# Where three top-k selections stand between one block's norm, its routing and the next stage in a 512-token decoder layer

## Chip, cores and metric

The kernel runs on one core of one Trainium2 chip. The metric is device time in microseconds, the median of several executions. TensorE (PE) multiplies, VectorE (DVE) and ScalarE (ACT) work elementwise, GpSimd (POOL) issues the indirect gathers, SyncE (SP) issues the plain loads.

## What is computed

One decoder layer on 512 tokens of width 1024: a mixing sublayer of sparse attention and a gated recurrence (HGRN2), then a feed-forward sublayer (PEER) in which each token picks 8 x 16 of 16384 single-neuron experts. The reference, cut to what matters here:

```python
# attention: each query keeps the 128 keys with the best indexer score
logits = relu(einsum('bqhd,bsd->bqhs', qi, k_idx))
score  = einsum('bqhs,bqh->bqs', logits, wi)
_, sel = top_k(where(causal, score, -inf), 128)
...
h = _layer_norm(ALPHA * x + concat([att_out, hg_out]) @ w_out, ln1_g, ln1_b)
# PEER
q = h @ w_q ; s = einsum('thpd,hpkd->thpk', q, sub_keys)
s_top, i_top = top_k(s, 16)
best, pos = top_k(pairwise sums of s_top, 16)        # -> experts, gates
hid = gelu(einsum('td,thkd->thk', x, u[experts]))
ffn = einsum('thk,thkd->td', softmax(best) * hid, v[experts])
x = _layer_norm(ALPHA * h + ffn, ln2_g, ln2_b)
```

## The kernel before

Tokens lie in four blocks of 128 (one token a partition). The mixing part runs in two stages, and the PEER part of the blocks is done in two ways.

`stage([0])` computes recurrence and attention of block 0, then index keys and index queries of blocks 1 to 3, `index_scores(1)`, the output projection with the first norm of block 0 (`mix_norm`), then `index_scores(2)` and `choose(1)`, `choose(2)`, then the queries and the top-k lists of block 0's PEER (`queries`, `routing`), which end in lists of indices `idx0_0` and `idx0_1` (line L622). `stage([1, 2, 3])` does the same for the other three blocks together: `index_scores(3)` and `choose(3)`, four recurrence projections (`hf`, `hq`, `hi`, `hg`), the recurrence block by block (`hgrn`), attention block by block, `mix_norm`, `queries`. After it blocks 2 and 3 go through a dense form of PEER that streams all experts, a loop over 128 key rows which TensorE bounds; block 1's experts are gathered beside it.

`index_scores(b)` has eight matmuls, eight copies on ScalarE (tile `rl`) and eight sums on DVE (L411) into the tile `isc`. `choose(b)` has 16 steps on that tile, each a MAX of eight values (L420) and a MATCH_REPLACE that marks them (L421), and a mask at the end; the tile is 256, 384 or 512 columns wide for block 1, 2 or 3. The attention of a block reads the mask with each head's scores (L443, tile `P`).

The PEER of block 0 gathers. A *row* is one expert slot for 128 tokens: POOL issues an indirect DMA of 128 x 1024 floats (L641, 0.524 MB) into one of nine buffers, and DVE takes the dot product with the block's tokens (L665, tile `gu`, 128 u rows) or adds the weighted row (L678, tile `gv`, 76 v rows). These 204 rows are handed out by `pump(n)`: whoever calls it puts the next n rows there in program order. Calls stand in `choose` (1 row at each step), between the loads of each projection (`PUMP` has the number by place), in the recurrence, between the heads of attention (4), in `mix_norm` (2) and in `queries`. While no rows are listed yet (all of stage 0) `pump` does nothing.

Instructions are issued in an order that a scheduler makes from the program and a cost model of its own. `tc.keep_in_program_order(ins)` pins one instruction: it stands behind whatever was written before it on its engine. Rows and many loads are pinned, most else is free, so the scheduler may move a selection step up or down past other work.

The norm (`layer_norm`) has sums, L143 (subtract the mean, times the weight), a root worked out in eleven small steps on 128 x 1 (L115 to L120), and L144 (times the root, plus the bias). Queries and routing of a block read its result, tile `hs`. In the section of rows, L131 is the sum for the norm, L493 the output projection, L525 the queries.

In the changed kernel four lines are added ahead, so L143 and L144 keep their numbers, the score sums are L411, MAX is L422, MATCH_REPLACE L425, attention's scores L447, a u row L669, a v row L682.

Of the kernel before, what the change touches and what calls it, by code (L numbers as in the profile page):

```python
# [15 lines left out]
ALU = mybir.AluOpType  # L16
# [16 lines left out]
STB = 6  # L33
PJ = 16

PUMP = {"cw": 0, "qi": 0, "hf": 4, "hq": 4, "hi": 4, "hg": 3, "qa": 2, "hgrn": 2, "att": 4, "mix": 2, "sel": 1,
        "q0": 7, "q1": 0, "q2": 0, "q3": 0}

PEK1 = 14
# [12 lines left out]
def tile_decoder_layer(ctx, tc, a, out):  # L52
    nc = tc.nc
# [32 lines left out]
    caus = pre.tile([128, 512], F32, name="caus")  # L86
# [184 lines left out]
    def hgrn(b, pr, mixT):  # L271
# [20 lines left out]
        if b:  # L292
            pump(PUMP["hgrn"])
        kt = k2(f"kt{b}")
# [104 lines left out]
        for i, b in enumerate(blocks):  # L399
            pr[b][key] = [t[:, i * 128:(i + 1) * 128] for t in ts_]  # L400

    def index_scores(b, pr):
        nk = (b + 1) * 128
        sc = pre.tile([128, 512], F32, name=f"isc{b}", tag="isc", bufs=3)[:, :nk]
        for h in range(8):
            ip = bank(f"ip{b}_{h}")
            lo = (h % 2) * 64
            nc.tensor.matmul(ip[:, :nk], pr["qi"][h // 2][lo:lo + 64, :], kiT[lo:lo + 64, :nk], start=True, stop=True)
            rl = k2(f"rl{b}_{h}")
            nc.scalar.activation(rl[:, :nk], ip[:, :nk], AF.Relu)  # L410
            nc.vector.scalar_tensor_tensor(sc, rl[:, :nk], pr["widx"][:, h:h + 1],  # L411
                                           caus[:, 512 - nk:] if h == 0 else sc, op0=ALU.mult, op1=ALU.add)
        return sc

    def choose(b, sc):

        m8 = pre.tile([128, 8], F32, name=f"m8_{b}", tag="m8", bufs=2)
        for i in range(16):
            pump(PUMP["sel"])
            nc.vector.max(m8, sc)  # L420
            nc.vector.match_replace(sc, m8, sc, GONE)  # L421
        nc.vector.tensor_scalar(sc, sc, -2e38, BIG, op0=ALU.is_gt, op1=ALU.mult)  # L422
        return sc
# [422 lines left out]
    def stage(blocks, xT):  # L846
        mixT = pre.tile([128, 8, 128 * len(blocks)], F32, name=f"mixT{blocks[0]}", tag="mixT",
                        padded_shape=[128, 8, 384])
        if blocks == [0]:
            pr = {}  # L850
# [8 lines left out]
            pens = {0: pen0}  # L859
        else:  # L860
            pr = index["pr"]
            pens = dict(index["sc"])
            pens[3] = choose(3, index_scores(3, pr[3]))
            kv_norm(blocks, pr)
            hp = hgrn_proj(blocks, xT)
        for i, b in enumerate(blocks):
# [10 lines left out]
            index["sc"] = {1: index_scores(1, index["pr"][1])}  # L877
        mix_norm(blocks, mixT)
        if blocks == [0]:
            index["sc"][2] = index_scores(2, index["pr"][2])  # L880
            for b in (1, 2):
                index["sc"][b] = choose(b, index["sc"][b])
        hT = pre.tile([128, 8, 128 * len(blocks)], F32, name=f"hT{blocks[0]}", tag="mixT",
                      padded_shape=[128, 8, 384])
        queries(blocks, hT)
# [13 lines left out]
    index = {}  # L899
# [55 lines left out]
```

## Time and profile before

| | before |
|---|---|
| time, median of 3 executions | 1598.87 us (1594.95 to 1606.39) |
| time of the profiled execution | 1608.33 us |
| its span | 1606.6 us |
| PE busy | 1450.4 us (90%) |
| DVE busy | 1385.0 us (86%) |
| ACT busy | 708.2 us (44%) |
| POOL busy | 672.9 us (42%) |
| DMA | 467.89 MB, mean 291 GB/s |

The page cuts the span into 40 slices of about 40 us and gives the busy share of an engine in each in tenths. Other views give the busy time of each engine in a stretch, groups of instructions of a line, the waits of an engine by what ended them, and a timeline. The places on the timeline that matter: block 0's norm at 122 to 136 us, its first gather at 197, attention of block 1 from 385 on, the output projection of blocks 1 to 3 from 491 to 521, their norms to 543.5, the dense loop from about 840 to the end.

### The profile page before, as it was taken

The page shows a single profiled execution, that of the slowest core. Times are in us where ns is not written, and L with a number is a line of the kernel's source. Part 1 is how long each engine was busy: PE and PEld are TensorE (multiplying, and loading weights), DVE is VectorE, ACT ScalarE, POOL GpSimd, SP SyncE. Part 2 cuts the span into 40 slices and gives each one's busy share as a digit, 9 for nine tenths or more (in the row PEclk, how much of TensorE's full clock was granted, in tenths as well). Part 3 has the DMA queues.
Part 4 walks back from the last instruction along what each step waited for, and adds up shares of the span by engine and source line. Part 5 has one row for each costly group of instructions (what it writes and reads, how often), then busy time and mean ns, then how long its engine had stood idle before and what let it go on. Part 6 is the DMA issues. An engine that isn't in the chain of part 4 may idle for free. (4 is left out here: it accounts for less than half of the span.)

```text
span 1606.6 us, 24502 instructions
## 1 busy us (share of the span) xinstructions
PE 1450.4 (90%) x7858; PEld 1088.9 (68%) x7858; DVE 1385.0 (86%) x3263; ACT 708.2 (44%) x1502; POOL 672.9 (42%) x531
## 2 busy tenths in 40 slices
PE   8997999757888599679989999999999999999996
PEld 4756544444443366246668888888888889988895
DVE  4219999789898989988887899998998899999998
ACT  3312321223430113169994555555555555555553
POOL 0000057858875610255433444444443344544440
PEclk9998999755799799899999999999999999999998
DMA  8445499889899860467778999999999999999995
GB/s 291 172 154 178 134 388 341 324 296 342 309 336 372 305 244 21 146 201 225 227 238 308 342 347 339 350 355 341 350 354 340 326 348 359 364 334 341 352 365 190
DMA packets 166161, 467.89 MB, mean 291 GB/s; under 512 B 18576, under 2 KB 18704, under 8 KB 165904
## 3 DMA queue, kind: packets, MB, share of 16 engines
q0 software_dynamic: 73728, 268.47, 48.0%
q1 hardware_dynamic: 92304, 197.86, 34.1%
q8 instruction: 62, 1.02, 0.2%
q14 instruction: 67, 0.55, 0.1%
HBM read 464.16 MB, written 2.10 MB: 290 GB/s over the span
## 5 line engine op out<-in xcount | busy, mean ns | idle before, releaser
L641 POOL DMA_INDIRECT gu<-in_u_dram,idx x256 | 328.5, 1283 | 423.4 <-DVE gu L665 212.5
L641 POOL DMA_INDIRECT gv<-in_v_dram,idx x256 | 333.8, 1304 | 401.4 <-DVE hs L678 226.8
L665 DVE SCALAR_TENSOR_TENSOR gu<-gu,hs 128x1024 f32<-128x1024 f32 x256 | 310.7, 1236 | 33.6 <-DMA gu<-in_u_dram,idx 32.6
L678 DVE SCALAR_TENSOR_TENSOR hs<-gv,gate,hs 128x1024 f32<-128x1024 f32 x204 | 261.5, 1282 | 13.5 <-DMA gv<-in_v_dram,idx 11.8
L774 ACT CAST v_0h<-v 128x512 fp32r<-128x512 f32 x128 | 79.7, 623 | 97.4 <-PE acc L805 58.5
L774 ACT CAST v_1h<-v 128x512 fp32r<-128x512 f32 x128 | 79.5, 621 | 93.1 <-DMA v<-in_v_dram 54.3
L525 PE MATMUL pq<-hT,wpq 128*128 128x128 f32 (+1 forms) x512 | 118.5, 389 | 0.0
L776 DVE TENSOR_TENSOR u_0l<-u,u_0h 128x512 fp32r<-128x512 f32 x128 | 88.5, 691 | 26.5 <-ACT u_0h L774 23.8
L774 ACT CAST u_0h<-u 128x512 fp32r<-128x512 f32 x128 | 79.3, 619 | 65.0 <-PE hp L785 34.0
L805 PE MATMUL acc<-v_0h,wl 128*128 128x512 f32 x256 | 102.0, 398 | 3.4 <-DVE wl L795 3.2
L776 DVE TENSOR_TENSOR v_1l<-v,v_1h 128x512 fp32r<-128x512 f32 x128 | 87.9, 687 | 18.6 <-ACT v_1h L774 18.0
L805 PE MATMUL acc<-v_0h,wh 128*128 128x512 f32 x256 | 101.0, 394 | 0.0
L525 PEld LDWEIGHTS pq<-hT,wpq 128*128 128x128 f32 x512 | 79.3, 196 | 31.9 <-issue 1.8
L774 ACT CAST u_1h<-u 128x512 fp32r<-128x512 f32 x128 | 79.4, 621 | 47.4 <-PE acc L805 41.0
L805 PE MATMUL acc<-v_1h,wl 128*128 128x512 f32 x256 | 99.9, 390 | 0.1
L805 PE MATMUL acc<-v_1h,wh 128*128 128x512 f32 x256 | 99.7, 389 | 0.0
L805 PE MATMUL acc<-v_0l,wh 128*128 128x512 f32 x256 | 99.5, 390 | 0.0
L776 DVE TENSOR_TENSOR u_1l<-u,u_1h 128x512 fp32r<-128x512 f32 x128 | 87.7, 685 | 5.0 <-ACT wh L793 3.0
L776 DVE TENSOR_TENSOR v_0l<-v,v_0h 128x512 fp32r<-128x512 f32 x128 | 88.2, 689 | 3.7 <-ACT v_0h L774 2.8
L785 PE MATMUL hp<-hTl,u_0h 128*128 128x256 f32 x512 | 83.8, 286 | 6.6 <-ACT u_0h L774 6.6
L785 PEld LDWEIGHTS hp<-hTl,u_0h 128*128 128x128 f32 x512 | 76.4, 189 | 19.3 <-ACT u_0h L774 10.9
L785 PE MATMUL hp<-hTh,u_1l 128*128 128x256 f32 x512 | 84.6, 287 | 5.1 <-DVE u_1l L776 4.9
(275 smaller groups left out, 3154.6 us busy)
## 6 DMA issues: line engine op xcount, KB each, us to landing
v<-in_v_dram SPq DMA_DIRECT2D x256, 256.0 KB, 5.9
u<-in_ut_dram SPq DMA_DIRECT2D x256, 256.0 KB, 6.0
wpq<-in_w_pq_dram SPq DMA_DIRECT2D x32, 512.0 KB, 4.9
wo<-in_w_o_dram SPq DMA_DIRECT2D x16, 512.0 KB, 5.3
hfw<-in_w_hf_dram SPq DMA_DIRECT2D x8, 512.0 KB, 4.9
hqw<-in_w_hq_dram SPq DMA_DIRECT2D x8, 512.0 KB, 5.4
hiw<-in_w_hi_dram SPq DMA_DIRECT2D x8, 512.0 KB, 6.3
qaw<-in_w_qa_dram SPq DMA_DIRECT2D x8, 512.0 KB, 5.8
```

The costliest lines, as they stand in the source:

```text
L525: nc.tensor.matmul(qp[:, :nt], w[:, k, :], hT[:, k, :nt], start=(k == 0), stop=(k == 7))
L641: nc.gpsimd.indirect_dma_start(out=t, out_offset=None, in_=table, in_offset=bass.IndirectOffsetOnAxis(ap=idx[b][k // 64][:, k % 64:k % 64 ...
L665: nc.vector.scalar_tensor_tensor(g, g, 1.0, hs[b], op0=ALU.mult, op1=ALU.mult, accum_out=hd[:, k:k + 1]))
L678: nc.vector.scalar_tensor_tensor(hs[b], g, gate[:, b, k:k + 1], hs[b], op0=ALU.mult, op1=ALU.add))
L774: nc.scalar.copy(h, x)
L776: nc.vector.tensor_tensor(l, x, h.bitcast(F32), op=ALU.subtract)
L785: nc.tensor.matmul(hp, ut[:, k * 128:(k + 1) * 128], ht[n][:, k, :], start=(n + q + k == 0), stop=(n == 1 and q == 2 and k == 3))
L805: nc.tensor.matmul(acc[i][n], wt[:, sl], vt, start=(j == 0 and q == 0), stop=(j == 127 and q == 2))
```

## The change

```diff
--- before.py
+++ after.py
@@ -33,7 +33,7 @@
 STB = 6
 PJ = 16
 
-PUMP = {"cw": 0, "qi": 0, "hf": 4, "hq": 4, "hi": 4, "hg": 3, "qa": 2, "hgrn": 2, "att": 4, "mix": 2, "sel": 1,
+PUMP = {"cw": 0, "qi": 0, "hf": 3, "hq": 3, "hi": 3, "hg": 3, "qa": 2, "hgrn": 2, "att": 4, "mix": 2, "sel": 1,
         "q0": 7, "q1": 0, "q2": 0, "q3": 0}
 
 PEK1 = 14
@@ -399,7 +399,7 @@
         for i, b in enumerate(blocks):
             pr[b][key] = [t[:, i * 128:(i + 1) * 128] for t in ts_]
 
-    def index_scores(b, pr):
+    def index_scores(b, pr, behind=False):
         nk = (b + 1) * 128
         sc = pre.tile([128, 512], F32, name=f"isc{b}", tag="isc", bufs=3)[:, :nk]
         for h in range(8):
@@ -408,16 +408,20 @@
             nc.tensor.matmul(ip[:, :nk], pr["qi"][h // 2][lo:lo + 64, :], kiT[lo:lo + 64, :nk], start=True, stop=True)
             rl = k2(f"rl{b}_{h}")
             nc.scalar.activation(rl[:, :nk], ip[:, :nk], AF.Relu)
-            nc.vector.scalar_tensor_tensor(sc, rl[:, :nk], pr["widx"][:, h:h + 1],
-                                           caus[:, 512 - nk:] if h == 0 else sc, op0=ALU.mult, op1=ALU.add)
+            ins = nc.vector.scalar_tensor_tensor(sc, rl[:, :nk], pr["widx"][:, h:h + 1],
+                                                 caus[:, 512 - nk:] if h == 0 else sc, op0=ALU.mult, op1=ALU.add)
+            if behind and h == 0:
+                tc.keep_in_program_order(ins)
         return sc
 
-    def choose(b, sc):
+    def choose(b, sc, behind=False):
 
         m8 = pre.tile([128, 8], F32, name=f"m8_{b}", tag="m8", bufs=2)
         for i in range(16):
             pump(PUMP["sel"])
-            nc.vector.max(m8, sc)
+            ins = nc.vector.max(m8, sc)
+            if behind and i == 0:
+                tc.keep_in_program_order(ins)
             nc.vector.match_replace(sc, m8, sc, GONE)
         nc.vector.tensor_scalar(sc, sc, -2e38, BIG, op0=ALU.is_gt, op1=ALU.mult)
         return sc
@@ -860,7 +864,8 @@
         else:
             pr = index["pr"]
             pens = dict(index["sc"])
-            pens[3] = choose(3, index_scores(3, pr[3]))
+            pens[2] = choose(2, pens[2], behind=True)
+            pens[3] = choose(3, index_scores(3, pr[3]), behind=True)
             kv_norm(blocks, pr)
             hp = hgrn_proj(blocks, xT)
         for i, b in enumerate(blocks):
@@ -877,9 +882,9 @@
             index["sc"] = {1: index_scores(1, index["pr"][1])}
         mix_norm(blocks, mixT)
         if blocks == [0]:
-            index["sc"][2] = index_scores(2, index["pr"][2])
-            for b in (1, 2):
-                index["sc"][b] = choose(b, index["sc"][b])
+
+            index["sc"][2] = index_scores(2, index["pr"][2], behind=True)
+            index["sc"][1] = choose(1, index["sc"][1], behind=True)
         hT = pre.tile([128, 8, 128 * len(blocks)], F32, name=f"hT{blocks[0]}", tag="mixT",
                       padded_shape=[128, 8, 384])
         queries(blocks, hT)
```

In words: (1) the first score sum of block 2 and the first selection step of block 1 are pinned, so that none of them is issued before block 0's norm is through. (2) The selection of block 2 moves from there to the start of the next stage, behind block 0's routing, and is pinned; since rows are listed by then, each of its 16 steps now calls for a row. The selection of block 3 is pinned behind it. (3) The three projections `hf`, `hq` and `hi` call for three rows a place in place of four: `hf` to `hi` give up twelve rows.

What this does to the issue order is seen at three places on DVE. The first is block 0's norm; `hs_104` is the block's tokens, `isc_695` and `isc_799` are the score tiles of blocks 1 and 2, `rs_tl`, `rs_yl` and `vel` belong to the root. Before:

```order
L143 SCALAR_TENSOR_TENSOR hs_104<-hs_104,mvl_0_777,ln_0_0_763 128x1024
L411 SCALAR_TENSOR_TENSOR isc_799<-rl_0_802,cw_619,caus 128x384
L420 MAX m_1_840<-isc_695 128x8
L115 TENSOR_SCALAR rs_tl_0_785<-vel_0_782 128x1
L411 SCALAR_TENSOR_TENSOR isc_799<-rl_1_807,cw_619,isc_799 128x384
L421 MATCH_REPLACE isc_695<-m_1_840,isc_695 128x256
L116 TENSOR_SCALAR rs_yl_0_784<-rs_tl_0_785 128x1
```

and after:

```order
L118 TENSOR_TENSOR rs_tl_0_785<-vel_0_782,rs_yl_0_784 128x1
L119 SCALAR_TENSOR_TENSOR rs_tl_0_785<-rs_tl_0_785,rs_yl_0_784 128x1
L120 SCALAR_TENSOR_TENSOR rs_yl_0_784<-rs_tl_0_785,rs_yl_0_784 128x1
L144 SCALAR_TENSOR_TENSOR hs_104<-hs_104,rs_yl_0_784,ln_0_1_765 128x1024
L411 SCALAR_TENSOR_TENSOR isc_799<-rl_0_802,cw_619,caus 128x384
L411 SCALAR_TENSOR_TENSOR isc_799<-rl_1_807,cw_619,isc_799 128x384
```

The score sums of block 2 and the selection of block 1 stood between the steps of the root; now the root's steps follow each other and L144 comes before the first score sum.

The second place is where attention of block 1 begins (tile `P`, its first head); `gu` are u rows of block 0 with their number behind the name, L327 and L328 are the recurrence. Before:

```order
L665 SCALAR_TENSOR_TENSOR gu_94_2144,hd_1466<-gu_94_2144,hs_104 128x1024
L328 TENSOR_TENSOR S_3_2557<-S_3_2557,ds_3_2548 128x256
L665 SCALAR_TENSOR_TENSOR gu_95_2147,hd_1466<-gu_95_2147,hs_104 128x1024
L351 TENSOR_TENSOR o_2566<-o_0_2569,gs_1929 128x4x64
L443 ISA P_0_2748,nmx_2743<-sp_0_2746,isc_695 128x256
```

and after:

```order
L328 TENSOR_TENSOR S_3_2569<-S_3_2569,ds_3_2560 128x256
L669 SCALAR_TENSOR_TENSOR gu_116_2391,hd_1391<-gu_116_2391,hs_104 128x1024
L669 SCALAR_TENSOR_TENSOR gu_117_2394,hd_1391<-gu_117_2394,hs_104 128x1024
L351 TENSOR_TENSOR o_2578<-o_0_2581,gs_1941 128x4x64
L447 ISA P_0_2760,nmx_2755<-sp_0_2758,isc_695 128x256
```

Rows are counted from 0: 96 stood ahead of the first score, now 118.

The third place is the norm of block 1 in the second stage (`hs_3192` before, `hs_3204` after; `mix` is the output projection, L496 or L500 adds it). Before, v rows of block 0 (`gv`) stand between the norms' steps, about every third instruction:

```order
L134 TENSOR_SCALAR vel_2_3343<-mvl_2_3338 128x1
L118 TENSOR_TENSOR rs_tl_1_3314<-vel_1_3311,rs_yl_1_3313 128x1
L143 SCALAR_TENSOR_TENSOR hs_3194<-hs_3194,mvl_2_3338,ln_1_0_3292 128x1024
L678 SCALAR_TENSOR_TENSOR hs_104<-gv_48_3262,gate,hs_104 128x1024
L115 TENSOR_SCALAR rs_tl_2_3346<-vel_2_3343 128x1
L119 SCALAR_TENSOR_TENSOR rs_tl_1_3314<-rs_tl_1_3314,rs_yl_1_3313 128x1
L496 SCALAR_TENSOR_TENSOR hs_3196<-hs_3196,mix_1_3360 128x512
L678 SCALAR_TENSOR_TENSOR hs_104<-gv_49_3265,gate,hs_104 128x1024
```

After:

```order
L500 SCALAR_TENSOR_TENSOR hs_3206<-hs_3206,mix_1_3340 128x512
L132 BN_AGGR mvl_1_3318<-stl_1_0_3319 128x2
L682 SCALAR_TENSOR_TENSOR hs_104<-gv_59_3301,gate,hs_104 128x1024
L131 BN_STATS stl_2_0_3351<-hs_3206 128x6
L134 TENSOR_SCALAR vel_1_3323<-mvl_1_3318 128x1
L143 SCALAR_TENSOR_TENSOR hs_3204<-hs_3204,mvl_1_3318,ln_1_0_3304 128x1024
L131 BN_STATS stl_3_0_3383<-hs_3208 128x6
L132 BN_AGGR mvl_2_3350<-stl_2_0_3351 128x2
```

The 60th v row (`gv_59`) is the last until the three norms are through. From the 60th v row to the end of the program DVE's order is otherwise that of before.

## Rows read from the trace of the kernel before

**Rows 1.** The page's part 2: TensorE's busy tenths in 40 slices of the span.
```profile
PE   8997999757888599679989999999999999999996
```
**Rows 2.** Stretches: length; PE, PEld, DVE, ACT, POOL busy (count); clock; DMA share; GB/s.
```profile
123.40:197.00 73.60, 59.43 (x354) 45.34 (x353) 73.60 (x368) 17.13 (x42) 0.00 (x0) 0.88 0.45 151
197.00:276.30 79.30, 78.47 (x255) 37.16 (x253) 73.21 (x159) 19.82 (x29) 49.11 (x43) 1.00 0.98 362
276.30:384.80 108.50, 71.96 (x529) 49.06 (x530) 94.65 (x190) 24.67 (x71) 78.46 (x64) 0.64 0.88 312
384.80:490.90 106.10, 86.70 (x288) 43.33 (x288) 96.70 (x168) 40.76 (x96) 83.52 (x70) 0.80 0.92 330
490.90:521.00 30.10, 29.36 (x64) 12.68 (x64) 23.70 (x29) 0.00 (x0) 13.56 (x12) 0.94 1.00 385
521.00:543.50 22.50, 4.01 (x17) 3.14 (x16) 22.22 (x54) 2.35 (x4) 14.02 (x10) 0.61 0.88 303
543.50:578.40 34.90, 34.71 (x119) 21.98 (x120) 28.06 (x25) 5.93 (x12) 20.62 (x18) 0.91 0.95 357
```
**Rows 3.** Timeline of DVE at block 0's norm: start, duration (us), instruction.
```profile
122.18 1.27 DVE L143 SCALAR_TENSOR_TENSOR hs<-hs,mvl,ln 128x1024 f32<-128x1024 f32 x1
134.65 1.27 DVE L144 SCALAR_TENSOR_TENSOR hs<-hs,rs_yl,ln 128x1024 f32<-128x1024 f32 x1
137.55 0.87 DVE L420 MAX8 m<-isc 128x8 f32<-128x384 f32 x2
139.26 0.87 DVE L420 MAX8 m<-isc 128x8 f32<-128x384 f32 x2
```
**Rows 4.** DVE's groups by shape, 123.4 to 197 us: count | busy us, mean ns.
```profile
L420 DVE MAX8 m<-isc 128x8 f32<-128x384 f32 x16 | 8.7, 546 | 0.0
L420 DVE MAX8 m<-isc 128x8 f32<-128x256 f32 x16 | 6.5, 407 | 0.0
```
**Rows 5.** Timeline of ACT and POOL: first query scores copied, first gather issued.
```profile
149.72 0.59 ACT L534 COPY pss<-psc 128x512 f32<-128x512 f32 x1 [2.64 <-PE psc L529]
197.38 1.15 POOL L641 DMA_INDIRECT gu<-in_u_dram,idx  x1 [120.12 <-DVE idx L622]
```
**Rows 6.** DVE's waits, 197 to 545 us: total us, times, longest.
```profile
DVE gu L665 <- DMA gu<-in_u_dram,idx: 13.0, 11, 2.9
DVE P L443 <- PE sp L441: 7.9, 8, 2.9
```
**Rows 7.** Rows and gathers by line: duration ns min/median/max, first and last start.
```profile
L665 DVE SCALAR_TENSOR_TENSOR gu<-gu,hs x59: 1209/1219/2974, 275.1 to 383.3; 128x1024 f32<-128x1024 f32 x59
L641 POOL DMA_INDIRECT gu<-in_u_dram,idx x112: 937/989/1988, 200.1 to 399.8; - x112
```
**Rows 8.** Timeline of DVE: first score, last rows, mixing output, rows between norms.
```profile
384.77 0.41 DVE L443 CUSTOM_DVE_ANT_0 P<-sp,isc 128x256 f32<-128x256 f32 x1
...
478.91 12.08 DVE L678 SCALAR_TENSOR_TENSOR hs<-gv,gate,hs 128x1024 f32<-128x1024 f32 x9
490.90 0.68 DVE L472 TENSOR_TENSOR mixT<-oT,rT 128x512 f32<-128x512 f32 x1
...
520.77 1.27 DVE L678 SCALAR_TENSOR_TENSOR hs<-gv,gate,hs 128x1024 f32<-128x1024 f32 x1
...
538.25 1.28 DVE L678 SCALAR_TENSOR_TENSOR hs<-gv,gate,hs 128x1024 f32<-128x1024 f32 x1
...
540.90 0.16 DVE L120 SCALAR_TENSOR_TENSOR rs_yl<-rs_tl,rs_yl 128x1 f32<-128x1 f32 x1
541.09 0.16 DVE L118 TENSOR_TENSOR rs_tl<-vel,rs_yl 128x1 f32<-128x1 f32 x1
...
542.26 1.28 DVE L144 SCALAR_TENSOR_TENSOR hs<-hs,rs_yl,ln 128x1024 f32<-128x1024 f32 x1
```
**Rows 9.** Timeline of PE: first transpose of the normed tokens, with its wait.
```profile
536.93 1.97 PE L213 MATMUL hT_ps<-ident,hs 128*128 128x128 f32 x8 [15.86 <-DVE rs_tl L115]
```

## The prediction

> **What bounds the kernel now.** I read the busy tenths of the page first, then the table of stretches, then the order of DVE, and last the timeline at the places where the order changes. TensorE is full from about the twentieth slice to the end [rows 1], and the 34.9 us in which the queries of blocks 1 to 3 start on TensorE hold 34.71 us of its work [rows 2]. From there on nothing in the change is left except four rows of block 0 that move ahead of that point, so a microsecond gained or lost before it is gained or lost at the end. I call that point N: the last normalized block of stage [1,2,3], 542.26 + 1.28 = 543.5 us [rows 8].
>
> Between block 0's norm and N the engine to watch is DVE. It is busy for 73.60 of 73.60 us up to the first gather, then 73.21 of 79.30, 94.65 of 108.50, 96.70 of 106.10, 23.70 of 30.10 and 22.22 of 22.50 [rows 2]. So 384.1 us of its work stand in 420.1 us, 36 us are idle, and the question of the whole change is whether N moves by more or less than the work and the idle time on this one engine. The idle time was ended mostly by gather DMAs (13.0 us for u rows) and by score matmuls (7.9 us) [rows 6]. Where TensorE waits, DVE is the releaser: before N it waits 15.86 us for the norms [rows 9].
>
> **Part 1: the norm of block 0 is freed.** Before, L143 stands at 122.18 and L144, which ends the norm, at 134.65 [rows 3], because the small steps of the inverse root are dealt out among block 2's score sums and the first selection steps. After, these stand alone. There are eleven, and where they run alone they follow each other at 541.09 − 540.90 = 0.19 us [rows 8], so L144 comes at about 123.45 + 11 × 0.195 + 0.2 = 125.8 instead of 134.65, some 9 us earlier, and TensorE's queries with it.
>
> Block 1's and block 2's selections alternate before: one pair of steps takes 139.26 − 137.55 = 1.71 us [rows 3]. Split by the durations of their MAX, 546 against 407 ns [rows 4], a step of block 2 is 0.98 us, and its sixteen steps 15.7 us. They leave the stretch up to the first gather, and about one step of block 3's selection (1.3 us) goes with them. Three things come back: 1.4 us of waiting inside the inverse root, about 3 us because the score sums and block 1's steps now depend on each other back to back, and a wait for the first query scores. ScalarE copies these until 149.72 + 0.59 = 150.3 [rows 5]; 9 us earlier is 141.3, and DVE is ready for them at about 139.5, so 2 us. The first list of indices, and the first gather, come 15.7 + 1.3 − 6.4 = 10.6 us earlier: about 186.8 instead of 197.38 [rows 5].
>
> **Part 2: the selection of block 2 goes in front of stage [1,2,3].** From the first gather to the start of block 1's attention DVE now has everything it had, plus that selection (15.7 us, and 0.7 for its start and its mask). The place of 276.3 is where attention's inputs are built; up to it two rows fewer are pumped, 38 to 36 (−2.3), and 2 us of block 3's selection fall on the far side. Work 73.2 + 15.7 + 0.7 + 1.3 − 2.3 − 2 + 1.6 for dependent steps = 88.2, idle 2 to 3 us (before 6.1: the selection steps fill part of what waited for gathers): 91. 186.8 + 91 = 277.8 against 276.3. The 10.6 us of part 1 are already spent: **+1.5**.
>
> **Part 3: more rows stand ahead of block 1's attention.** This carries the sum. The sixteen rows that the moved selection pumps exceed the twelve that the three projections give up, and the scheduler packs them early: ahead of the first score of block 1, at 384.77 [rows 8], stood 96 rows, now 118. In 276.3 to 384.8 that is 59 rows before and 83 after, 24 more, at 1.219 us, the median of a u row [rows 7]: 29.3 us. With 2.7 us of block 3's selection behind 276.3, DVE's work is 94.65 + 32 = 126.6 us. The idle time of this stretch was 13.9 us, and rows now fill most of it; I keep 2.4 (bounds 0 and 13.9). So 129 instead of 108.5, **+20.5**; block 1's attention starts at 407 instead of 385.
>
> Can the gathers keep up? A row is 0.524 MB; 83 rows and about 3.5 MB of weights are 47 MB. The best rate that a stretch shows is 385 GB/s [rows 2], which gives 122 us, just under the 126.6 of DVE. In the Trainium skill, "DMA: Bandwidth & Descriptors", section "Where 436 GB/s comes from", the ceiling of the fabric is 435 GB/s; by that the same bytes would take an estimated 108 us and the sum stays as it is. No stretch here comes above 385.
>
> **Part 4: what is given back.** From block 1's first score to the last block's attention output (490.90 [rows 8]) 54 rows stand instead of 66. Almost all that go are in block 3's attention. But there the last nine rows (478.91, 12.08 us [rows 8]) run beside a chain over TensorE and ScalarE which ends only 0.9 us before the output does, so dropping them gains that 0.9 and perhaps 3 us of single rows that stand between two scores: **−4** (bounds −8 and +2). The output projection then is TensorE's, 29.36 of 30.10 [rows 2]; it has about four more rows beside it with the DMA share already 1.00, 4 × 0.524 MB / 385 GB/s = 5.4 us at worst, nothing at best: **+2**. Last, ten rows between 520.77 and 538.25 [rows 8] stand among the three norms behind the projection; after, all rows of this place are ahead of the last sum, and the norms run alone: ten rows less, 12 us: **−12**. Behind N there are 16 rows instead of 20 beside TensorE's queries, which are not waiting for them: 0 (to −2).
>
> Sum: 1.5 + 20.5 − 4 + 2 − 12 = **+8 us** at N, and at the end. A second way: DVE has 384.1 us before and four more rows (4.7 us) plus 5 us of dependent steps after, with an idle time of 36 before and 34 after: +8 as well, and with idle of 27 to 45, −1 to +19. The profiled execution took 1608.3 us by its own time, 0.6% above the median of 1598.9; 8 us on the median are 1607.
>
> Two ACT table loads fall away and the input loads of the three blocks go some places earlier on SP's queue. ScalarE is busy 24.67 of 108.50 us where it matters [rows 2], so this costs nothing; if attention waited for ScalarE, the loads would be worth 2 to 3 us together.
>
> **Rivals.**
> - *Faster.* The 22 extra rows ahead of block 1's attention cost only what was idle there: if DVE's idle 13.9 us take twelve of them and the TensorE work of that stretch (71.96 us at a clock of 0.64 [rows 2]) sets the pace, part 3 is +5 to 10 in place of 20.5, and N comes 3 to 8 us early; with block 3's attention closing up fully (−8) and no loss in the projection, 10 to 16 early. It decides once the stretch takes under 118 us. Against it: the 32 us are counted from the order, and the idle time was made by score and gather waits which don't vanish. Time 1583 to 1596.
> - *Slower.* The gathers starve. A gather issue takes 937 ns at best, 989 in the median and 1988 at worst, and a u row up to 2974 ns where it waits behind something [rows 7]. With the selection steps now between the rows, issues may come at 1.4 us a row and more, and the 83 rows of part 3 then take 83 × 1.4 = 116 us where 83 × 1.219 = 101 are counted: +15 on top. It decides when the rows' mean spacing exceeds 1.3 us. POOL has 78.46 busy of 108.50 [rows 2], which leaves room, so it is less likely. The Trainium skill, "SBUF — State Buffer", section "SBUF: two separate sides", says that DVE in a two-port mode or with two SBUF inputs shuts GpSimd out of the shared pair for a whole instruction, which delays descriptors; by that rule a denser DVE makes issues slower. The longest issue above fits it, but the median says that it is rare. Time 1615 to 1630.
> - *The change doesn't do what it says.* TensorE's queries are not ready when DVE is, the first gather stays near 192 to 197, and part 2 is +7 to +12 rather than +1.5. Against it: the queries' weights are loaded by then, and the scores were waiting for the norm. Time 1612 to 1618.
>
> **How the numbers follow.** The forecast (N later by 2 to 14 us) has 0.50; N within −6 and +2, since attention closes up more, 0.17; the faster rival 0.10; starved gathers 0.15; late queries 0.08. The time is that of the forecast, 1607 (its own range 1601 to 1613). The range of 1591 to 1624 leaves 0.08 below and 0.08 above. A measurement here can tell about 1% from no change, 16 us, so faster has 0.07 (below 1583: most of the faster rival's lower half), slower 0.22 (above 1615: starved gathers, and the upper edge of forecast and late queries), the same 0.71.
>
> **What would show it.** Part 1: L144 of block 0 near 126 and the first gather near 187. Part 2: the place of 276.3 at 277 to 279. Part 3: the first score of block 1 near 407, with DVE over 95% busy in the 110 us before. Part 4: the time from the last projection matmul to N at 10 to 11 us instead of 22. If the first score of block 1 comes before 397, part 3 was too dear and the faster rival is at work; if gather waits ahead of it exceed 15 us, the slower one. N compared with the end tells whether what lies behind N really only shifts.

## The result, and the profile of the changed kernel

The changed kernel takes 1621.7 us (median of 4 executions, 1616.35 to 1629.42) beside 1596.91 us (4 executions, 1594.08 to 1606.39) for the kernel before: a ratio of 1.0142, 95% interval 1.0106 to 1.0178, so 17 to 28 us slower. The forecast was 1607 and slower, the range reached to 1624. The sign and the range held; the size did not: 24.8 us were lost where 8 were forecast, and "slower", by more than 1%, had a chance of only 0.22.

The profiled executions are 1606.6 and 1620.5 us long, 13.9 us apart. The table of stretches of the changed kernel, with cuts at the same events as [rows 2] (the columns are those of [rows 2]; the fifth stretch is the fifth and sixth there, and the sixth runs from the last norm to the last list of indices, 157.70 us before):

```profile
123.40:185.70 62.30, 58.46 (x357) 44.52 (x356) 59.55 (x315) 17.09 (x42) 0.00 (x0) 0.97 0.53 179
185.70:276.20 90.50, 87.60 (x284) 42.62 (x282) 87.61 (x198) 18.95 (x28) 49.58 (x47) 1.00 0.90 328
276.20:410.40 134.20, 65.27 (x508) 46.09 (x508) 121.81 (x246) 25.60 (x73) 100.14 (x79) 0.55 0.90 321
410.40:517.40 107.00, 82.84 (x282) 42.73 (x278) 85.70 (x137) 38.71 (x92) 71.15 (x60) 0.83 0.87 305
517.40:559.40 42.00, 31.41 (x80) 15.35 (x80) 36.67 (x71) 2.36 (x5) 19.62 (x16) 0.89 0.83 313
559.40:714.90 155.50, 137.80 (x444) 76.41 (x445) 140.99 (x816) 37.17 (x71) 39.57 (x32) 0.96 0.45 148
```

The first three stretches are those of block 0's norm and queries, of the rows up to attention's inputs, and of the rows up to block 1's first score. The first is 11.3 us shorter than before, the second 11.2 longer, the third 25.7 longer; DVE is still 91% busy in it. Attention (the fourth) takes 107.0 us beside 106.1, though DVE has 11 us less to do in it, so its idle time there grew from 9.4 to 21.3 us. Projection and norms are 10.6 us shorter. The last normalized block of stage [1,2,3] ends at 559.4 instead of 543.5.

From the timelines of DVE and POOL, the events that the prediction named (start, duration, instruction):

```profile
125.82 1.28 DVE L144 SCALAR_TENSOR_TENSOR hs<-hs,rs_yl,ln 128x1024 f32<-128x1024 f32 x1
185.73 1.26 POOL L645 DMA_INDIRECT gu<-in_u_dram,idx  x1 [108.12 <-DVE pos L576]
410.44 0.41 DVE L447 CUSTOM_DVE_ANT_0 P<-sp,isc 128x256 f32<-128x256 f32 x1
517.45 0.69 DVE L476 TENSOR_TENSOR mixT<-oT,rT 128x512 f32<-128x512 f32 x1 [5.57 <-ACT rT L108]
558.14 1.28 DVE L144 SCALAR_TENSOR_TENSOR hs<-hs,rs_yl,ln 128x1024 f32<-128x1024 f32 x1
```

Beside [rows 3], [rows 5] and [rows 8]: block 0's norm is 8.8 us earlier, the first gather 11.6 us earlier, block 1's first score 25.7 us later. Before block 3's last sum DVE waits 5.57 us for a chain over TensorE and ScalarE; before, that wait was 0.3 us, since nine rows lay beside the chain.

DVE's waits in the third stretch (total us, times, longest), before and then after:

```profile
DVE gu L665 <- DMA gu<-in_u_dram,idx: 7.4, 6, 2.9
DVE qs L291 <- ACT e L290: 3.0, 2, 2.6
DVE AT L312 <- PE at L310: 2.5, 2, 2.2
```
```profile
DVE gu L669 <- DMA gu<-in_u_dram,idx: 11.5, 12, 6.5
```

The waits for ScalarE's `e` and TensorE's `at`, steps of the recurrence, fall from 5.5 us to 0.2, so rows do fill those; but DVE now waits 4.1 us longer for the rows' own gathers, and the idle time of the stretch stays (13.9 us before, 12.4 after). More than half of the gather waits is one wait, right behind the selection of block 3:

```profile
294.40 1.22 DVE L669 SCALAR_TENSOR_TENSOR gu<-gu,hs 128x1024 f32<-128x1024 f32 x1 [6.47 <-DMA gu<-in_u_dram,idx]
```

The u rows of the third stretch after, and the issues of block 0's u gathers from 185 to 420 us (duration in ns, min/median/max; first and last start):

```profile
L669 DVE SCALAR_TENSOR_TENSOR gu<-gu,hs x83: 1209/1218/1294, 275.1 to 409.0; 128x1024 f32<-128x1024 f32 x83
L645 POOL DMA_INDIRECT gu<-in_u_dram,idx x128: 932/1026/1986, 185.7 to 418.6; - x128
```

83 rows stand there, as counted from the order, with the duration that was taken for them, though in a row they start every 1.15 us (294.40, 295.55, 296.70). A gather's issue takes 1026 ns in the median beside 989 [rows 7].

### The profile page after: what moved, and what is told of

Same layout as the page of the kernel before. It is cut to its first block, busy times and chain, and to the rows that moved or that the text cites. A ratio compares the mean times of both kernels' runs of the same rounds, so it can differ in the third digit from the quotient of the medians.

```text
span 1620.5 us, 24509 instructions
## 1 busy us (share of the span) xinstructions
PE 1444.2 (89%) x7858; PEld 1090.8 (67%) x7858; DVE 1386.9 (86%) x3263; ACT 706.4 (44%) x1500; POOL 676.0 (42%) x531
## 5 line engine op out<-in xcount | busy, mean ns | idle before, releaser
L645 POOL DMA_INDIRECT gv<-in_v_dram,idx x256 | 339.8, 1327 | 415.9 <-DVE hs L682 251.8
L682 DVE SCALAR_TENSOR_TENSOR hs<-gv,gate,hs 128x1024 f32<-128x1024 f32 x204 | 261.2, 1280 | 11.3 <-DMA gv<-in_v_dram,idx 9.3
L700 PE MATMUL pw<-gv,dg 128*128 128x512 f32 x152 | 75.3, 618 | 14.0 <-ACT dg L698 9.7
```

The costliest lines, as they stand in the source:

```text
L645: nc.gpsimd.indirect_dma_start(out=t, out_offset=None, in_=table, in_offset=bass.IndirectOffsetOnAxis(ap=idx[b][k // 64][:, k % 64:k % 64 ...
L682: nc.vector.scalar_tensor_tensor(hs[b], g, gate[:, b, k:k + 1], hs[b], op0=ALU.mult, op1=ALU.add))
L700: nc.tensor.matmul(p[i], dg, g[:, i * 512:(i + 1) * 512], start=(k == ks[0]), stop=(k == ks[-1]))
```

## The experiments

Three milestones are read from each profile: the first score of block 1, the end of the last norm, and the last list of indices (the last DVE step of the routing of blocks 1 to 3, before which DVE is the engine that is full). "Rows ahead" are block 0's rows in front of the first score, counted in the issue order. "Work" and "idle" are DVE's busy and idle time from 123.4 us to the last list, summed over the stretches. Ratios are to the kernel before on the same chip; e7, e10 and e11 were executed once. The milestones are those of one execution each, and they scatter where the order is the same: with the order of before up to there (before, e3, e10, e12) the first score lies between 383.2 and 386.2, with that of the changed kernel (changed, e6, e7, e11) between 410.4 and 415.9.

| kernel | rows ahead | first score | attention | last norm | last list | work, idle | ratio (95%) |
|---|---|---|---|---|---|---|---|
| before | 96 | 384.8 | 106.1 | 543.5 | 701.2 | 530, 47 | 1 |
| before, once more (e10) | 96 | 383.2 | 117.9 | 552.8 | 710.5 | 530, 57 | |
| changed | 118 | 410.4 | 107.0 | 559.4 | 714.9 | 532, 59 | 1.0142 (1.0106 to 1.0178) |
| changed, once more (e11) | 118 | 415.5 | 106.9 | 565.0 | 718.8 | 532, 63 | |
| e1 no pins | 93 | 368.4 | 106.4 | 537.4 | 692.8 | 526, 44 | 0.9998 (0.9967 to 1.0029) |
| e2 late pins only | 121 | 409.2 | 104.5 | 555.7 | 709.5 | 529, 57 | 1.0132 (1.0067 to 1.0198) |
| e3 projections 3 only | 96 | 385.3 | 104.4 | 531.4 | 696.0 | 526, 46 | 1.0009 (0.9970 to 1.0048) |
| e4 no rows in selection 2 | 106 | 402.5 | 97.6 | 542.5 | 707.7 | 529, 55 | 1.0067 (1.0031 to 1.0102) |
| e5 early pins only | 102 | 386.3 | 103.7 | 541.0 | 696.1 | 530, 43 | 1.0027 (0.9990 to 1.0064) |
| e6 more rows in attention | 118 | 415.9 | 109.7 | 571.1 | 724.5 | 533, 68 | 1.0154 (1.0106 to 1.0201) |
| e7 no rows in attention | 118 | 410.6 | 97.2 | 549.8 | 713.9 | 516, 75 | |
| e8 selections in attention | 93 | 353.2 | 156.3 | 552.3 | 709.9 | 536, 50 | 1.0154 (1.0096 to 1.0212) |
| e9 fewer rows ahead | 100 | 396.1 | 126.0 | 567.6 | 724.4 | 534, 67 | 1.0161 (1.0114 to 1.0208) |
| e12 no rows in norms | 96 | 386.2 | 111.1 | 541.0 | 704.0 | 532, 49 | 1.0029 (0.9996 to 1.0062) |

### Which part of the change costs the time

**e1, the move without the pins.**

```diff
-            pens[2] = choose(2, pens[2], behind=True)
-            pens[3] = choose(3, index_scores(3, pr[3]), behind=True)
+            pens[2] = choose(2, pens[2], behind=False)
+            pens[3] = choose(3, index_scores(3, pr[3]), behind=False)
...
-            index["sc"][2] = index_scores(2, index["pr"][2], behind=True)
-            index["sc"][1] = choose(1, index["sc"][1], behind=True)
+            index["sc"][2] = index_scores(2, index["pr"][2], behind=False)
+            index["sc"][1] = choose(1, index["sc"][1], behind=False)
```

> The changed kernel without its pins: the selection of block 2 is written at the start of the next stage and calls for rows, the projections call for three, but nothing is held back. In the issue order the selection then stands where it stood in the kernel before, ahead of the first gather, with 93 rows ahead of block 1's first score (96 before, 118 after). Theory A (rows ahead of block 1's attention set when the last norm ends): first gather near 197, first score near 381, the last norm ends near 543 to 546, time within 6 us of the kernel before (1591 to 1603). Theory B (the moved selection's rows and the smaller numbers in the projections cost something by themselves): slower than before by 10 us or more.

The ratio is 0.9998 and the last norm ends at 537.4. Without a pin the scheduler puts the selection back ahead of the first gather, so writing it elsewhere and calling for rows there costs nothing by itself. Theory B falls. The first score came at 368.4, 13 us earlier than theory A had worked out; the gain was gone by the dense loop (the first matmul of its hidden layer starts at 837.9, and at 839.0 in the kernel before), so it was not worth anything.

**e2, the late pins alone, and e5, the early pins alone.**

```diff
 e2
-            index["sc"][2] = index_scores(2, index["pr"][2], behind=True)
-            index["sc"][1] = choose(1, index["sc"][1], behind=True)
+            index["sc"][2] = index_scores(2, index["pr"][2])
+            index["sc"][1] = choose(1, index["sc"][1])
 e5
-            pens[2] = choose(2, pens[2], behind=True)
-            pens[3] = choose(3, index_scores(3, pr[3]), behind=True)
+            pens[2] = choose(2, pens[2])
+            pens[3] = choose(3, index_scores(3, pr[3]))
```

> The changed kernel with only the selections of blocks 2 and 3 pinned; block 2's score sums and block 1's selection are free again, so the steps of block 0's norm are dealt out among them as before. 121 rows stand ahead of block 1's first score (118 in the changed kernel). Theory A: the late pins make the loss, first score near 412, last norm ends near 560, time near 1620. Theory B (the loss comes from the early pins, which make the sums and block 1's steps dependent back to back): first score near 390, time near 1600.

> The changed kernel with only block 2's score sums and block 1's selection pinned; the selections of blocks 2 and 3 are free, and in the issue order they stand ahead of the first gather again. 102 rows stand ahead of block 1's first score (118 in the changed kernel, 96 in the kernel before). Theory A (DVE's work from block 0's norm to the last list of indices is the same in every version, 526 to 532 us, and what differs is its idle time: 44 to 48 us where the late pins are missing, 55 to 59 where they are): idle 44 to 50, last list of indices at 698 to 706, time within 0.5% of the kernel before. Theory B (the early pins cost as much as the late ones): last list near 710, time 0.8% or more above the kernel before.

The first score of e2, from DVE's timeline (386.27 in e5):

```profile
409.17 0.41 DVE L447 CUSTOM_DVE_ANT_0 P<-sp,isc 128x256 f32<-128x256 f32 x1
```

The late pins alone bring the first score to where it stands in the changed kernel, and the time to 1.0132; the early pins alone leave both nearly where they were (1.0027). In e5 block 0's norm ends even earlier than in the changed kernel (L144 starts at 123.44), yet block 2's selection and parts of block 3's are ahead of the first gather again, which comes at 203.2, later than before. Whether the pin of block 2's or that of block 3's selection does it, no run separates. Over all timed kernels: where the selections of blocks 2 and 3 are held behind the first gather (changed, e2, e4, e6, e8, e9) the ratio lies between 1.0067 and 1.0161; where they are not (e1, e3, e5, e12) it lies between 0.9998 and 1.0029.

**e3, the projections' numbers alone.**

```diff
-PUMP = {"cw": 0, "qi": 0, "hf": 4, "hq": 4, "hi": 4, "hg": 3, ...
+PUMP = {"cw": 0, "qi": 0, "hf": 3, "hq": 3, "hi": 3, "hg": 3, ...
```

> The kernel before with only the three projections' numbers changed from 4 to 3. The order up to block 1's first score is the same (96 rows ahead); 60 instead of 66 rows stand in attention, none between the last norms, 32 instead of 20 behind them. Theory A: first score at 384 to 385, attention stays at 106 us since a chain over TensorE and ScalarE sets it, the last norm ends 9 us earlier (near 534), and 12 rows more behind it give 5 to 9 of it back: time 1590 to 1598. Theory B (every row costs its 1.2 us wherever it stands): last norm 15 us earlier and the whole of it given back, 1597.

The ratio is 1.0009. The last norm ends 12 us earlier, between the 9 and the 15 of the two theories, and most of it is given back behind it: from the last norm to the last list are 164.6 us in place of 157.7, and from there to the dense loop 140.5 in place of 137.8. Up to block 1's first score the order is the same: the scheduler packs rows early, and the rows that the projections give up are missing at the end of the stage, not in the projections.

### How the late pins cost it

**e4, no rows in the moved selection.**

```diff
-            pump(PUMP["sel"])
+            pump(PUMP["sel"] if b != 2 else 0)
```

> The changed kernel, but block 2's selection calls for no rows. 106 instead of 118 rows stand ahead of block 1's first score, 50 in attention, 32 instead of 16 behind the last norm. Theory A: first score 12 rows earlier, near 396, last norm ends near 545, 16 rows more behind it give back 5 to 10: time 1610 to 1616. Theory B (gathers starve on the selection's steps, the number of rows doesn't matter): first score stays near 408 to 410, time near 1621 or above.

12 rows fewer ahead, and the first score 8 us earlier than in the changed kernel (12 x 1.22 = 14.6 had been expected): 402.5. The time falls to 1.0067. DVE's work from the first gather to the first score is 12.4 us less, its idle time 3.2 us more, and the first gather comes 1.3 us later. The first score follows the number of rows ahead of it, though not by the full price of each; the theory that gathers starve, by which it would have stayed where it was, explains at most the rest. The last norm ends at 542.5, a little earlier than before (543.5), and the kernel is still slower; 32 rows stand behind that norm, and from the last norm to the last list it takes 165.2 us in place of 157.7.

**e7, no rows called for in attention.**

```diff
-PUMP = {... "hgrn": 2, "att": 4, "mix": 2, ...
+PUMP = {... "hgrn": 2, "att": 0, "mix": 2, ...
```

> The changed kernel with no rows called for in attention: 30 rows stand there, which the recurrence and the projection of attention's queries called for, instead of 54. Theory A (a chain over TensorE, ScalarE and small DVE steps sets attention's time): 95 to 104 us from the first score to the last block's output. Theory B (rows set it): 107 - 24 x 1.27 = 76 us.

97.2 us: theory A. By block, in the table of stretches (columns of [rows 2]), e7 and then the kernel before:

```profile
410.60:439.00 28.40, 18.66 (x64) 10.13 (x65) 25.84 (x60) 13.24 (x36) 22.75 (x21) 0.67 0.97 361
439.00:473.50 34.50, 29.08 (x106) 14.82 (x105) 22.43 (x33) 11.62 (x27) 17.17 (x15) 0.90 0.75 273
473.50:507.80 34.30, 30.03 (x112) 14.34 (x110) 7.63 (x20) 13.34 (x29) 0.61 (x1) 1.00 0.02 8
```
```profile
384.80:413.70 28.90, 22.55 (x77) 12.00 (x79) 27.56 (x72) 11.86 (x36) 23.24 (x21) 0.56 0.96 358
413.70:449.20 35.50, 29.59 (x106) 14.70 (x104) 30.26 (x56) 15.15 (x31) 29.54 (x22) 0.91 0.88 295
449.20:490.90 41.70, 34.57 (x112) 16.63 (x110) 38.88 (x44) 13.75 (x29) 30.74 (x29) 0.88 0.93 339
```

Block 3's attention holds 26 rows before and none in e7. That takes 31.2 us from DVE, which is then busy 7.63 of 34.30 us, and shortens the stretch by only 7.4 us; blocks 1 and 2 (17 and 13 rows in e7, 19 and 21 before) are 0.5 and 1.0 us shorter. So a row in block 3's attention costs about 0.3 us instead of 1.22. This is a rough price: over the executions block 3's stretch takes 33.4 us with 11 rows (e4), 39.1 to 40.7 with 12 to 20 (changed, e2, e3, e9, e11), and 39.4 to 44.0 with 25 or 26 (before, e1, e5, e6, e12), once 49.5 (e10). A row that the late pins move from there to a place ahead of attention turns about 0.3 us into the 1.2 that it adds to DVE's work. The one execution of e7 took 1637.31 us, though its last list comes 1.0 us earlier than the changed kernel's: 40 rows are left behind the last norm, and some of them behind the last list too.

**e6, more rows in attention.**

```diff
-PUMP = {... "hgrn": 2, "att": 4, "mix": 2, ...
+PUMP = {... "hgrn": 2, "att": 6, "mix": 2, ...
```

> The changed kernel with six rows called for in each half of a block's attention, in place of four. Up to the last block's attention the order is the same (118 rows ahead of block 1's first score); then ten more rows stand in attention and 4 instead of 16 behind the last norm. Theory A (rows in attention fill DVE time that is idle there anyway): attention takes 107 to 110 us, the last norm ends at 559 to 563, the last list of indices comes at 703 to 708 (714.9 in the changed kernel), time 0.3 to 0.9% above the kernel before. Theory B (a row costs its 1.2 us wherever it stands): attention 119 us, last norm 572, last list again at 714, time 1.3% or more above the kernel before.

Half of this held. Ten rows more made attention 2.7 us longer (109.7), as theory A has it, and DVE's idle time in it fell from 21.3 to 12.5 us. The time was not better but 1.0154. The rows were taken from the place behind the last norm, where four of sixteen were left, and there they had been nearly free too: DVE's idle time from the last norm to the last list rose from 14.5 to 27.9 us and the stretch stayed at 153.4 (155.5). The rest of the 11.7 us by which the last norm is later came at the first score (5.5 us later in the same order) and in projection and norms (3.5 us).

**e9, all pins, fewer rows ahead.**

```diff
-PUMP = {... "hf": 3, "hq": 3, "hi": 3, ... "att": 4, ...
+PUMP = {... "hf": 0, "hq": 0, "hi": 0, ... "att": 9, ...
```

> The changed kernel with all its pins, but the three projections call for no rows and each half of a block's attention for nine. 100 rows stand ahead of block 1's first score (118 in the changed kernel, 96 before), 64 in attention (54, 66), 22 behind the last norm (16, 20). Theory A (the loss is the rows that the late pins pull ahead of attention, not the moved selections): first score at 386 to 392, attention 104 to 109 us, last norm at 536 to 544, DVE's idle time up to the last list 44 to 50 us, time within 0.5% of the kernel before. Theory B (the pinned selections in front of the stage cost it by themselves): first score at 400 or later, last norm at 550 or later, time 0.8% or more above the kernel before.

Theory A's numbers fell: 396.1 at the first score is between the two forecasts, attention took 126 us, and the last norm (567.6) and the time (1.0161) are where theory B had them. Of the 126 us most went into the first block's stretch, which is shown here and for the changed kernel:

```profile
396.10:446.10 50.00, 21.66 (x71) 10.60 (x71) 38.91 (x88) 11.30 (x33) 37.85 (x29) 0.57 0.84 284
```
```profile
410.40:439.90 29.50, 18.57 (x65) 9.85 (x62) 25.90 (x61) 13.30 (x36) 23.55 (x22) 0.67 0.96 349
```

28 rows stand in block 1's attention (17 in the changed kernel). DVE was already busy for 25.90 of 29.50 us there, so 11 rows more (13 us of work) come on top, and 7.5 us of new waiting with them. Block 1's attention is no cheap place, and e9 put only 20 rows into that of block 3 against 26 before. So fewer rows ahead are no cure by themselves. That it matters where they go instead fits these stretches, but theory B, that the pinned selections cost something whatever the rows do, is not excluded by this run: with both selections behind the first gather no placing of rows was found that costs nothing.

**e8, the selections ahead of the blocks that use them.**

```diff
-            pens[2] = choose(2, pens[2], behind=True)
-            pens[3] = choose(3, index_scores(3, pr[3]), behind=True)
+            pens[3] = index_scores(3, pr[3])
...
         for i, b in enumerate(blocks):
+            if b == 2 or b == 3:
+                pens[b] = choose(b, pens[b], behind=True)
             attention(b, pr[b], pens[b], mixT[:, 0:4, i * 128:(i + 1) * 128])
...
-            pump(PUMP["sel"])
+            pump(0)
```

> The early pins as in the changed kernel, but the selections of blocks 2 and 3 are written right ahead of the attention of block 2 and of block 3, pinned there and without rows; the projections call for four rows again, attention for six. 93 rows and neither selection stand ahead of block 1's first score; 24 rows stand behind the last norm. Theory A (attention has idle DVE time that other work can take): first score at 345 to 358, attention 125 to 132 us, last norm at 520 to 532, last list of indices at 688 to 698, time 0.2 to 1% below the kernel before. Theory B (selection ahead of each block holds the chain of that block): attention 140 us or more, last norm at 540 or later, time equal to or above the kernel before.

The first score comes at 353.2, as worked out, and attention takes 156.3 us: theory B. Selection is no filler there: DVE is busy for 144.1 of the 156.3 us, and each block's scores stand behind its selection. The last norm ends at 552.3.

**e12, no rows among the last norms.**

```diff
-PUMP = {... "att": 4, "mix": 2, ...
+PUMP = {... "att": 4, "mix": 1, ...
```

> The kernel before with one row in place of two at each load of the output projection. Order and rows up to the projection are those of before (96 ahead, 66 in attention); none instead of ten stand among the last three norms and 28 instead of 20 behind them. Theory A (rows behind the last norm are free up to about twenty, those among the norms are not): last norm 10 to 12 us earlier, 532 to 534, last list 2 to 6 us earlier, time 0 to 0.4% below the kernel before. Theory B (rows behind the norm cost what they save): last list where it was, time the same.

The time is 1.0029 with an interval that takes in 1: no gain. Projection and norms fall from 52.6 to 43.7 us, 8.9 us for eight rows, and from the last norm to the last list 163.0 us stand in place of 157.7. The first half is near what the prediction used, the second what e3 showed as well: 28 rows behind the norm are more than are free there. The last norm itself ends at 541.0 and not at 532 to 534, because attention took 111.1 us in this execution, in the order in which it took 106.1.

**e10 and e11, the two kernels once more.**

> The kernel before, once more, for its stretches on the chip of these runs. All theories: first score at 383 to 388, last norm at 541 to 546; from the last list of indices to the dense loop 144 to 146 us if the longer stretch there belongs to the chip, 138 if it belongs to the orders that were tried.

> The changed kernel, once more, on the same chip. First score at 408 to 416, last norm at 557 to 565, DVE's idle time from block 0's norm to the last list 55 to 62 us by theory A; by a theory that the idle time is chance from one execution to the next, anywhere from 44 to 62.

The changed kernel's idle time is 63 us (59 in the first execution), just above both forecasts, that of the kernel before 57 (47). The first score of e10 came as expected, its last norm (552.8) did not: the kernel before had one event in this execution that the first had not (last section), worth about 8 us in attention. From the last list to the dense loop it took 138.8 us, 137.8 in the first. That doesn't clear the chip of the 144 to 146 us of some experiments: the longer stretches are all on the chip of e5 to e8 (143.8 to 146.1) and in e1 and e2, and on the chip of e9 to e12 none is longer than 138.8. What makes them is open.

So idle times of single executions are uncertain by ten microseconds, as large as the difference that they are to explain. What repeats in the two pairs is the first score, 25.7 and 32.3 us later. Attention does not repeat: the changed kernel's took 107.0 and 106.9 us, that of the kernel before 106.1 and 117.9, and 111.1 in e12, which has the same rows up to there. The verdict on causes rests on the timed ratios.

## Why the prediction was right, and where it was short

**Part 1 was right.** L144 was put at 125.8 and stands at 125.82; the first gather was put at 186.8 and is at 185.73. The terms that were worked out for the score sums and block 1's steps add up to the place of the first gather within 1.1 us, and the rival in which the queries hold the gather back, with the gather at 192 to 197, is out.

**Part 2 was right.** The inputs of attention were put at 277.8, and are there at 276.2. The 11 us gained by the early gather are spent on the moved selection, as forecast; the loss does not come from here.

**Part 3 had the mechanism and missed the idle time.** Block 1's first score was put 22 us later and is 25.7 later (32.3 in the second pair). The rows were counted right, 83 at 1.218 us. DVE's work is 121.8 us (126.6 forecast), but its idle time is 12.4 us where 2.4 had been kept, and this is the step that failed: the prediction let more rows fill the waits of this stretch. They fill those of the recurrence (5.5 us to 0.2), but the rows' own waits for gathers grow instead, from 7.4 us to 11.5, and the idle time stays where it was. In the last 110 us before the score DVE is 95% busy, as was said; 7.1 of the 12.4 us lie in the 24 us before these. This repeats: with the order of the changed kernel the stretch has 12.4 to 14.5 us of idle time, 11.5 to 13.5 of them for gathers (changed, e6, e7, e11), with that of before 12.3 to 13.9, of which 0 to 8.2 are for gathers (before, e3, e10, e12). In each of the first four one wait of 4.5 to 6.5 us stands right behind block 3's selection; what holds that gather up is open.

The slower rival, starving gathers, is thus in part at work. Its sign was more than 15 us of gather waits ahead of the first score: 13.9 us in the first execution of the changed kernel, 17.8 in the second (13.0 and 8.8 in the kernel before). Its reason, slower issues, is not seen as an effect of the change: in the third stretch the median issue is 1177 ns beside 1118 before. The Trainium skill ("SBUF — State Buffer", section "SBUF: two separate sides") lets DVE with two SBUF inputs and a GpSimd instruction that reads SBUF hold a shared port pair only in turn, for a whole instruction. The traces agree in direction and not in size: of block 0's u gathers those whose issue runs for four fifths of its time or more beside a row take 1177 ns in the median (51 of 128), those that meet no row 936 (15), though DVE is busy beside most of these too; before, 1171 (47) and 941 (19). So an issue beside a row is some 240 ns longer (160 and 280 in e10 and e11), less than the 1.22 us of a row, and it is so in both kernels.

The 385 GB/s that the prediction took as the best rate of any stretch is no limit either: the page of the kernel before has 388 in one slice, and e1 moved more over a long stretch (last section). The prediction's reason for the rows ahead was wrong as well: it set the sixteen rows of the selection against the twelve of the projections, while e3 has the same 96 rows ahead with the twelve gone, and from e1 to e2 the late pins alone move them from 93 to 121.

**Part 4 came out in part by luck.** Attention was to give back 4 us (bounds −8 and +2). The measured term is +0.9 in the first pair and −11.0 in the second, of which 7.8 are the event of the last section, so these executions don't settle it. The trace had shown a reason against more than 0.9, a chain over TensorE and ScalarE that ends within 0.9 us of the last rows, and the prediction quoted it; the 3 us of single rows between scores were hoped for without a row for them. By the price of e7, about 0.3 us a row, the eleven rows that leave block 3 would be 3 us. Projection and norms were put at −10 together and are −10.6, but neither term is right: the projection, put at +2, is 1.6 us shorter (28.5 us from 517.4 to its last matmul's end at 545.9, against 30.1), and the norms, put 12 us shorter, are 9.0 shorter (13.5 us where 10 to 11 were expected). The two errors cancel. Behind the last norm 0 to −2 was forecast and −2 came.

The sum of the working was +8 us at the last norm; measured are +15.9 in the first pair, outside the 2 to 14 of the forecast, and +12.2 in the second. In the first the difference is 5.2 us in part 3 and 4.9 us in attention, less 1.6 and 0.6 us in the other parts. The second way of the prediction, work plus idle time, had the same fault: it kept DVE's idle time ahead of the last norm at 34 us, and it is 44.7.

That the last norm tells the end held for the change itself (+15.9 there, +13.9 at the end). It is no rule: in e4 the last norm is 1.0 us earlier than before and the profiled execution 10.3 us longer, with 32 rows behind that norm instead of 20.

**What stays open.** The profiled pairs differ by 13.9 and 9.7 us, the timed medians by 24.8. In both pairs the profiled execution of the kernel before lies above its median (1608.3 to 1596.9, 1615.1 to 1610.1), that of the changed kernel near its own in the first (1622.4 to 1621.7). This accounts for the gap by numbers; where the time lies in the executions without a profile, no run shows, and that 1621.7 still falls into the range, 2.3 us from its end, is owed to the width of the range and not to the sum. That the late pins cost the time is shown (e2 beside e1 and e5); how the loss divides into rows ahead of attention, gather waits and what lies behind the last norm is argued from single executions. Nor was a version found that beats the kernel before: the best ratio is 0.9998 (e1).

## What to carry to other kernels

When one engine does both filler work and the small steps of a chain that runs over other engines, count the filler by place. In front of the chain a row costs its full duration of that engine's work (12 rows were 12.4 us of work in e4, 7.9 us of them at the first score). Beside the chain it costs a quarter of it or less: about 0.3 us a row for 26 rows in block 3's attention, and next to nothing behind the last norm up to 16 rows (153.4 us to the last list with 4 rows in e6, 153.8 to 155.5 with 16 in both executions of the changed kernel; 157.7 with 20 before, 163.0 with 28 in e12). An edit that starts the filler earlier and pulls it ahead of such a chain exchanges cheap places for dear ones, and a stretch that gives up cheap rows gets little shorter.

A pin that holds a free piece of work behind something changes the order of all filler around it; print the order, count the filler ahead of each chain in it, and forecast from that count, with idle time kept as it is in the trace unless a row says what ends it: work that fills one wait may lengthen another.

## What the runs showed of the hardware that was not expected

In the second execution of the kernel before (e10), TensorE, ScalarE and DVE all came nearly to rest in block 3's attention while the DMA queues ran at 416 GB/s. Two neighbouring stretches of it, columns as in [rows 2]:

```profile
466.00:472.00 6.00, 5.54 (x14) 2.68 (x12) 5.86 (x5) 2.15 (x4) 4.76 (x5) 0.72 1.00 386
472.00:478.70 6.70, 0.45 (x2) 0.00 (x0) 1.77 (x2) 0.59 (x1) 2.97 (x3) 0.88 1.02 416
```

and the instruction that went on, a copy on ScalarE, with its wait, which the trace puts to nothing on this core's engines:

```profile
478.08 0.59 ACT L461 COPY ols<-ol 128x512 f32<-128x512 f32 x1 [7.12 <-remote]
```

Block 3's attention took 7.8 us more than in the first execution (49.5 us from 451.6 to 501.1, against 41.7), in the same order of instructions. What the copy waited for isn't in the trace. The rate alone is not it: in the first execution the same place ran at 416 and 403 GB/s (466.0 to 472.0 and 472.0 to 478.7) with DVE busy for 11.31 of the 12.70 us.

Nor is 385 GB/s the most that a longer stretch reaches. In e1, from the first gather to attention's inputs:

```profile
195.00:270.00 75.00, 73.38 (x241) 34.58 (x239) 73.51 (x161) 19.83 (x29) 51.64 (x44) 1.00 1.01 397
```

The stretches of the changed kernel that are 90 us and longer stay at 328 and below, at DMA shares up to 0.90.
